# Where the products of a two-layer diffusion backbone stand in PSUM: pairs for gate and up, single banks for the rest

## The chip, the cores and the metric

The kernel runs on one core of one Trainium2 chip. The metric is the device time of one execution in microseconds (us). Before the change three runs gave 3039.61, 3045.07 and 3048.42 us, a median of 3045.07 us. The engines are TensorE (PE, with its weight loads as PEld), VectorE (DVE), ScalarE (ACT), GpSimd (POOL) and SyncE (SP, which issues DMAs).

## The reference

Two layers over 512 latent tokens (X) and 256 context tokens (C) of width 1024, in fp32. Each layer: a half-step SwiGLU feed-forward (FFN), a token mixer, a second FFN. Layer 0 mixes by a gated convolution and a Fourier transform, layer 1 by attention, in which only X goes on after.

```python
def macaron_ffn(h, m, g, w_in, w_out, slot):
    xm = modulate(h, g[2 * slot], m[:, :, 3 * slot], m[:, :, 3 * slot + 1])   # rmsnorm, scale, shift
    y = swiglu(xm, w_in, w_out)            # (silu(x @ w_gate) * (x @ w_up)) @ w_out, D_FF = 2816
    return h + FFN_RES * m[:, :, 3 * slot + 2] * rmsnorm(y, g[2 * slot + 1])
...
q_x = attn_queries(u[..., :Q_COLS], g_q_mla[o], w_uq[o], rope_da, rope_mla)
kv_x = attn_keys_values(u[..., Q_COLS:], g_kv_mla[o], w_uk[o], w_uv[o], rope_da, rope_mla)
kv_c = attn_keys_values(xc @ w_in[:, Q_COLS:], g_kv_mla[o], w_uk[o], w_uv[o], None, None)
```

## The kernel before

Activations lie feature by feature: a stream has eight tiles of 128 features by its tokens, X of 512 columns, C of 256. In the last FFN the two halves of X are streams of their own, A and B, of 256 columns. Every fp32 product is made of three matmuls on high and low parts (`mm3`, L212 to L214), and each weight tile is split into its high part on ScalarE (L140) and its low part on VectorE or GpSimd (L142).

PSUM has eight banks, given out by three pools: `mm`, three single banks (L103); `pr`, two pairs of banks (L109); `st`, one bank for sums (L106). A tile that asks for a bank of a full pool waits until the last reader of the oldest tile is done.

In an FFN the 22 feature tiles f are worked in six blocks. For each f, `gate_up` (L393) makes a gate and an up product, 48 matmuls, and `activated` (L413) turns them into an act: silu on ScalarE (L416), the product on VectorE (L417), then the split into a high part on ScalarE (L219) and a low part on VectorE (L220), which is the last reader of the banks. X's two products take a `pr` pair. C's, A's and B's take the two halves of one `mm` bank, except in the leading tiles. `out_proj` (L474) makes a block's share of the down projection in `mm` banks, copied by ScalarE (L488) in block 0 and added by VectorE (L490) later. Acts have five buffers per stream. In three of the four FFNs (`AHEAD` 4) one stream makes the acts of f = 0 to 5 before the other begins, and `out_proj` of block 0 follows both, so that the sixth act, f = 5, waits for a buffer that block 0 frees.

Between the layers' parts, `post` (L309) adds the normed result to the stream and `pre` (L292) makes the modulated rows for the next part, one row for each of the eight tiles. `scratch` (L226) gives each row its place in PSUM: an `mm` bank for lane c (C and B), halves of a `pr` pair for lane x (X and A). A row of `pre` is one step on VectorE (L303), one on ScalarE (L304) and one on VectorE (L305). `lead4` (L422) then starts the next FFN on the first two feature tiles as the rows come.

In the attention layer `latents` makes the low-rank queries (`q_lat`), the queries of group 0 (`da_qk(0, "q")`), the low-rank keys (`kv_lat`, which needs C's rows) and more. The work of groups 1 to 3 is laid between the steps of the attention of the group before, by gaps of a set length (`GAP`).

The program is written by generators that advance with TensorE's work; a scheduler then sets the order on each engine, and each engine runs its instructions in that order. The adaLN products (L366) are put on VectorE beside the FFNs.

Of the kernel before, what the change touches and what calls it, by code (L numbers as in the profile page):

```python
# [18 lines left out]
P = 128  # L19
D = 1024  # L20
KT = D // P
# [8 lines left out]
LEAD = 2  # L30
# [9 lines left out]
LEAD0 = 2  # L40
# [35 lines left out]
class Builder:  # L76
# [149 lines left out]
    def scratch(self, s, k, keep=False):  # L226


        if s.lane == "c":
            return self.mm()[:, :s.n]  # L230
        if k == 0 or k % 2 == 0 and not keep:
            s.scr = self.pr()
        return s.scr[:, k % 2 * 512:k % 2 * 512 + s.n]
# [58 lines left out]
    def pre(self, s, st, A, B):  # L292

        nc = self.nc
        rb = yield from self.rnorm(s, st, D)
        with self.tc.high_priority(PRIORITY):
            s.xm = [self.pre_tile(s, k, A, B, rb) for k in range(KT)]

    def pre_tile(self, s, k, A, B, rb):
# [9 lines left out]
    def post(self, s, st, A, want_stats=True):  # L309
# [6 lines left out]
        for k in range(KT):  # L316
            with self.tc.high_priority(PRIORITY):
                t = self.scratch(s, k)
# [103 lines left out]
    def lead4(self, s, ws, lead=None):  # L422
# [6 lines left out]
        lead = lead or LEAD  # L429
# [6 lines left out]
    def lead_gate_up(self, s, ws, acts, lead=None):  # L436
        pss = self.lead4(s, ws, lead)
        for f in range(2):
            self.act(s, f, pss[2 * f], pss[2 * f + 1], acts)
# [54 lines left out]
    def ffn(self, l, i, s0, s1, done, ahead=0, extra=False):  # L494
# [23 lines left out]
        if ahead:  # L518
            for s in both:
# [3 lines left out]
                else:  # L523
                    items.append((gu(0) + gu(1), lambda *ws, s=s: self.lead_gate_up(s, ws, acts, LEAD0)))
# [249 lines left out]
    def da_qk(self, g, which):  # L774
# [14 lines left out]
        def both(wa, wb):  # L789
            pa, pb = self.proj(X, [(wa, P, 0), (wb, P, 0)], KT, X.xm)  # L790
# [37 lines left out]
    def latents(self):  # L828
# [48 lines left out]
        items += self.da_qk(0, "q")  # L877
# [336 lines left out]
    def attention(self, X, C, A, B, close_xm, done):  # L1214
# [61 lines left out]
        for g in range(1, 4):  # L1276
            items += self.da_qk(g, "q") + self.da_qk(g, "k") + self.da_v(g)
# [31 lines left out]
def body(tc, io, stop=99):  # L1309
    nc = tc.nc  # L1310
    with ExitStack() as es:
# [92 lines left out]
        def step(l, slot, l2, slot2):  # L1404
            def gen(s, st):
                b.norms += 1
                new = yield from b.post(s, st, b.par[l, cname[s], 3 * slot + 2])
                yield from b.pre(s, new, b.par[l2, cname[s], 3 * slot2 + 1], b.par[l2, cname[s], 3 * slot2])
# [63 lines left out]
        items += b.mixer(X, C, step(0, 1, 0, 2))  # L1472
# [5 lines left out]
        if stop > 3:  # L1478
            items += b.ffn(1, 0, X, C, step(1, 0, 1, 1), AHEAD2)
        if stop > 4:  # L1480
# [11 lines left out]
            items += b.attention(X, C, A, B, close_xm, step(1, 1, 1, 2))  # L1492
# [139 lines left out]
```

## Time and profile before

| | |
|---|---|
| median of three runs | 3045.07 us |
| profiled execution | 3044.23 us, span 3042.4 us |
| PE busy | 2895.1 us, 95% |
| DVE, ACT, POOL busy | 54%, 35%, 27% |
| share of PE in the chain of waits | 80% |

The trace's names leave the buffer numbers out: `pr<-xm` is a product into a pair, `mm<-act` a down projection. "Idle before" is the time for which an engine stood still ahead of an instruction, and what ended it. The stages: ffn(0,0) to about 610 us, the mixer to 880, ffn(0,1) to 1455, ffn(1,0) to 2030, attention to 2625, the last FFN to the end.

### The profile page before, as it was taken

The page shows a single profiled execution, that of the slowest core. Times are in us where ns is not written, and L with a number is a line of the kernel's source. Part 1 is how long each engine was busy: PE and PEld are TensorE (multiplying, and loading weights), DVE is VectorE, ACT ScalarE, POOL GpSimd, SP SyncE. Part 2 cuts the span into 40 slices and gives each one's busy share as a digit, 9 for nine tenths or more (in the row PEclk, how much of TensorE's full clock was granted, in tenths as well). Part 3 has the DMA queues.
Part 4 walks back from the last instruction along what each step waited for, and adds up shares of the span by engine and source line. Part 5 has one row for each costly group of instructions (what it writes and reads, how often), then busy time and mean ns, then how long its engine had stood idle before and what let it go on. Part 6 is the DMA issues. An engine that isn't in the chain of part 4 may idle for free.

```text
span 3042.4 us, 44263 instructions
## 1 busy us (share of the span) xinstructions
PE 2895.1 (95%) x17842; PEld 2559.9 (84%) x17842; DVE 1652.7 (54%) x3026; ACT 1049.8 (35%) x1740; POOL 812.8 (27%) x439
## 2 busy tenths in 40 slices
PE   5899999999999999999999999997999999989998
PEld 4788888878888888888788888886798878889998
DVE  7865665675475434345745333366367757623335
ACT  5332112444343221124421122244355556542223
POOL 4221111332242111114311111142433422622122
PEclk9999999999999999999999999998999999999999
DMA  7743333333234322233333333352876674532224
GB/s 260 238 154 129 121 130 127 126 101 123 106 140 146 111 90 91 90 113 117 118 126 110 131 111 125 104 158 97 270 173 182 175 188 102 182 125 91 98 98 139
DMA packets 189807, 412.14 MB, mean 135 GB/s; under 512 B 58337, under 2 KB 83553, under 8 KB 189602
## 3 DMA queue, kind: packets, MB, share of 16 engines
q1 hardware_dynamic: 126642, 372.05, 36.5%
q0 software_dynamic: 62960, 37.27, 5.7%
q8 instruction: 140, 2.29, 0.3%
q14 instruction: 65, 0.53, 0.1%
HBM read 374.09 MB, written 35.00 MB: 134 GB/s over the span
## 4 chain that ended last, share of the span: by engine, by line
PE 80%; DVE 7%; issue 4%; DMA 4%; ACT 3%; POOL 2%; SPq 0%; ACTq 0%; DVEq 0%; POOLq 0%
PE mm L212 17%; PE mm L213 16%; PE mm L214 16%; PE pr L213 9%; PE pr L214 9%; PE pr L212 9%; DVE junk L366 1%; PE pr L997 1%; ACT wh L140 1%; DMA dr<-stg 1%; PE mm L1006 1%; DVE wl L142 1%; POOL wl L142 1%; DVE xm L305 1%; DMA ot<-dr 1%
## 5 line engine op out<-in xcount | busy, mean ns | idle before, releaser
L142 POOL TENSOR_TENSOR wl<-wraw,wh 128x1024 fp32r<-128x1024 f32 (+1 forms) x274 | 666.3, 2435 | 1966.4 <-ACT wh L140 1928.2
L140 ACT ACTIVATE wh<-wraw 128x1024 fp32r<-128x1024 f32 (+2 forms) x474 | 492.2, 1040 | 979.2 <-PE mm L213 664.7
L212 PE MATMUL mm<-xm,wh 128*128 128x256 f32 (+1 forms) x1992 | 588.3, 297 | 22.9 <-DVE xm L305 9.0
L214 PE MATMUL mm<-xm,wl 128*128 128x256 f32 (+1 forms) x1992 | 589.5, 296 | 9.4 <-DVE wl L142 9.4
L213 PE MATMUL mm<-xm,wh 128*128 128x256 f32 (+1 forms) x1992 | 588.6, 295 | 0.0
L213 PE MATMUL pr<-xm,wh 128*128 128x512 f32 (+1 forms) x1328 | 510.2, 384 | 17.3 <-POOL xm L1446 9.6
L212 PE MATMUL pr<-xm,wh 128*128 128x512 f32 (+1 forms) x1328 | 507.8, 383 | 14.8 <-ACT xm L304 7.7
L214 PE MATMUL pr<-xm,wl 128*128 128x512 f32 (+1 forms) x1328 | 506.4, 381 | 3.7 <-POOL wl L142 3.7
L212 PE MATMUL mm<-act,wh 128*128 128x256 f32 (+1 forms) x1408 | 459.2, 327 | 17.0 <-ACT y L488 11.6
L213 PE MATMUL mm<-act,wh 128*128 128x256 f32 (+1 forms) x1408 | 457.3, 325 | 0.2
L214 PE MATMUL mm<-act,wl 128*128 128x256 f32 (+1 forms) x1408 | 456.9, 325 | 0.0
L212 PEld LDWEIGHTS mm<-xm,wh 128*128 128x128 f32 x1992 | 377.5, 190 | 36.4 <-DVE xm L305 9.5
L214 PEld LDWEIGHTS mm<-xm,wl 128*128 128x128 f32 x1992 | 377.3, 189 | 18.9 <-DVE wl L142 10.0
L213 PEld LDWEIGHTS mm<-xm,wh 128*128 128x128 f32 x1992 | 379.3, 190 | 11.1 <-DVE xm L305 2.1
L366 DVE CUSTOM_DVE_ANT_0 junk<-wmod,cond 128x1024 bf16<-128x1024 f32 x256 | 374.8, 1464 | 6.4 <-DMA wmod<-in_w_mod_dram 4.2
L142 DVE TENSOR_TENSOR wl<-wraw,wh 128x1024 fp32r<-128x1024 f32 x200 | 251.1, 1255 | 227.6 <-ACT wh L140 224.9
L213 PEld LDWEIGHTS pr<-xm,wh 128*128 128x128 f32 x1328 | 252.3, 190 | 76.0 <-DVE xm L305 15.7
L212 PEld LDWEIGHTS pr<-xm,wh 128*128 128x128 f32 x1328 | 252.4, 190 | 71.7 <-ACT xm L304 15.8
L212 PEld LDWEIGHTS mm<-act,wh 128*128 128x128 f32 x1408 | 266.4, 190 | 48.4 <-ACT y L488 17.2
L214 PEld LDWEIGHTS pr<-xm,wl 128*128 128x128 f32 x1328 | 252.5, 190 | 53.9 <-POOL wl L142 4.1
L213 PEld LDWEIGHTS mm<-act,wh 128*128 128x128 f32 x1408 | 268.9, 191 | 25.4 <-DVE act L220 1.7
L214 PEld LDWEIGHTS mm<-act,wl 128*128 128x128 f32 x1408 | 266.8, 189 | 23.5
(241 smaller groups left out, 3467.8 us busy)
## 6 DMA issues: line engine op xcount, KB each, us to landing
wraw<-in_w_ffn_in_dram SPq DMA_DIRECT2D x250, 512.0 KB, 3.5
wmod<-in_w_mod_dram SPq DMA_DIRECT2D x160, 512.0 KB, 3.8
wraw<-in_w_ffn_out_dram SPq DMA_DIRECT2D x104, 512.0 KB, 3.5
dr<-stg SPq DMA_DIRECT2D x40, 512.0 KB, 3.5
wraw<-in_w_in_even_dram SPq DMA_DIRECT2D x32, 512.0 KB, 3.5
qs<-dr POOLq DMA_DIRECT2D x56, 256.0 KB, 12.0
dr<-stg SPq DMA_DIRECT2D x36, 256.0 KB, 6.3
ks<-dr POOLq DMA_DIRECT2D x24, 384.0 KB, 10.8
```

The source lines that it names most:

```text
L140: self.nc.scalar.activation(out=h, in_=r, func=AF.Copy)
L142: eng.tensor_tensor(out=l, in0=r, in1=h.bitcast(F32), op=ALU.subtract)
L212: mmul(out, w[0], x[0], start=first, stop=False)
L213: mmul(out, w[0], x[1], start=False, stop=False)
L214: mmul(out, w[1], x[0], start=False, stop=last)
L305: nc.vector.scalar_tensor_tensor(out=x[:, 1], in0=t, scalar=B[:, k:k + 1], in1=x[:, 0].bitcast(F32), op0=ALU.add, op1=ALU.subtract)
L366: dot = nc.vector.tensor_tensor_reduce(out=junk, in0=w, in1=self.cond[n], op0=ALU.mult, op1=ALU.add, scale=1.0, scalar=0.0, accum_out=par[ ...
L997: self.nc.tensor.matmul(ps[:, c0:c1], q, k[:, c0:c1], start=i == 0, stop=i == len(passes) - 1)
L1006: self.nc.tensor.transpose(ps[:, kt * P:(kt + 1) * P], w[:, (k0 + kt) * P:(k0 + kt + 1) * P], self.ident)
```

## The change

It has four parts.

1. `gate_up` takes a `pr` pair for every stream.
2. `scratch` gives a row an `mm` bank by default; one pair for all eight rows is taken only in the posts of X after the mixer, of C after ffn(1,0) and of A after the attention, and in the pres of X and C after ffn(1,0).
3. `lead4` takes the first two feature tiles interleaved: tile 0 row by row, with the first three rows of tile 1 laid between, where before it made tile 0 whole and then tile 1.
4. The queries of group 1 are made right behind those of group 0, ahead of `kv_lat`, and both are projected into a `pr` pair (the last argument of `proj`).

```diff
-LEAD = 2
+LEAD = 3
...
-LEAD0 = 2
...
-    def scratch(self, s, k, keep=False):
-        if s.lane == "c":
+    def scratch(self, s, k, pair):
+        if not pair:
             return self.mm()[:, :s.n]
-        if k == 0 or k % 2 == 0 and not keep:
+        if k == 0:
             s.scr = self.pr()
         return s.scr[:, k % 2 * 512:k % 2 * 512 + s.n]
...
-        t = self.scratch(s, k, True)
+        t = self.scratch(s, k, pair)
...
     def gate_up(self, s, f, ws, acts):
         nc = self.nc
-        if s.n == 512:
-            ps = self.pr()
-            g, u = ps[:, :512], ps[:, 512:]
-        else:
-            ps = self.mm()
-            g, u = ps[:, :s.n], ps[:, s.n:2 * s.n]
+        ps = self.pr()
+        g, u = ps[:, :s.n], ps[:, 512:512 + s.n]
...
-        for i in range(0, 4, lead):
-            for k in range(KT):
-                for o, w in zip(pss[i:i + lead], ws[i:i + lead]):
-                    self.mm3(o, self.wk(w, k), s.xm[k], k == 0, k == KT - 1)
+        order = [(0, 0)]
+        for k in range(1, KT):
+            order += [(0, k)] + ([(2, k - 1)] if k <= LEAD else [])
+        order += [(2, k) for k in range(LEAD, KT)]
+        for i, k in order:
+            for o, w in zip(pss[i:i + 2], ws[i:i + 2]):
+                self.mm3(o, self.wk(w, k), s.xm[k], k == 0, k == KT - 1)
...
-            pa, pb = self.proj(X, [(wa, P, 0), (wb, P, 0)], KT, X.xm)
+            pa, pb = self.proj(X, [(wa, P, 0), (wb, P, 0)], KT, X.xm, which == "q" and g < 2)
...
-        items += self.da_qk(0, "q")
+        items += self.da_qk(0, "q") + self.da_qk(1, "q")
...
-            items += self.da_qk(g, "q") + self.da_qk(g, "k") + self.da_v(g)
+            items += (self.da_qk(g, "q") if g > 1 else []) + self.da_qk(g, "k") + self.da_v(g)
...
-        def step(l, slot, l2, slot2):
+        def step(l, slot, l2, slot2, posts=(), pres=()):
...
-        items += b.mixer(X, C, step(0, 1, 0, 2))
+        items += b.mixer(X, C, step(0, 1, 0, 2, (X,)))
...
-            items += b.ffn(1, 0, X, C, step(1, 0, 1, 1), AHEAD2)
+            items += b.ffn(1, 0, X, C, step(1, 0, 1, 1, (C,), (X, C)), AHEAD2)
...
-            items += b.attention(X, C, A, B, close_xm, step(1, 1, 1, 2))
+            items += b.attention(X, C, A, B, close_xm, step(1, 1, 1, 2, (A,)))
```

The order on the engines shows what becomes of this. On TensorE, C's six products in ffn(0,1): names with `pr` are pairs, with `mm` single banks, and the number tells tiles apart; `[waits ...]` names the engines waited for. Before:

```order
4875 L212 MATMUL pr_8210<-xm_7904,wh_8125 128x256 [waits DVE_49]
...
4923 L212 MATMUL mm_8344<-xm_7904,wh_8320 128x256 [waits Activation_49]
...
4936 L212 MATMUL pr_8211<-xm_7904,wh_8198 128x256 [waits DVE_49]
...
5019 L212 MATMUL mm_8417<-xm_7904,wh_8332 128x256 [waits Activation_49]
...
5067 L212 MATMUL mm_8484<-xm_7904,wh_8405 128x256 [waits Activation_49]
...
5115 L212 MATMUL mm_8551<-xm_7904,wh_8472 128x256 [waits DVE_49,Activation_49]
...
5163 L212 MATMUL mm_8626<-act_7846,wh_8539 128x512 [waits DMAHW4_49,DVE_49,Activation_49]
```

and now:

```order
4877 L211 MATMUL pr_8225<-xm_7919,wh_8140 128x256 [waits DVE_49]
...
4925 L211 MATMUL pr_8226<-xm_7919,wh_8213 128x256 [waits DVE_49]
...
4973 L211 MATMUL pr_8359<-xm_7919,wh_8335 128x256 [waits DVE_49]
...
5021 L211 MATMUL pr_8432<-xm_7919,wh_8347 128x256 [waits DVE_49]
...
5069 L211 MATMUL pr_8499<-xm_7919,wh_8420 128x256 [waits DVE_49]
...
5117 L211 MATMUL mm_8641<-act_7861,wh_8554 128x512 [waits DMAHW4_49,Activation_49]
...
5130 L211 MATMUL pr_8566<-xm_7919,wh_8487 128x256 [waits DVE_49]
...
5178 L212 MATMUL mm_8663<-act_7861,wh_8554 128x512
```

Before, C's third to sixth products stood in `mm` banks and the third began ahead of the second's; now the six are in pairs and each begins with a wait for VectorE, and the sixth has moved behind the first down projections.

On VectorE, the rows of X's `pre` in front of ffn(1,0): `h` is the stream, `xm` the row. Before:

```order
1422 L303 SCALAR_TENSOR_TENSOR pr_12240<-h_109,par_7946,st_12234 128x512 [waits PE_49]
...
1425 L305 SCALAR_TENSOR_TENSOR xm_12239<-pr_12240,par_9214,xm_12239 128x512 [waits Activation_49]
1426 L303 SCALAR_TENSOR_TENSOR pr_12240<-h_111,par_7946,st_12234 128x512 [waits DVE_49]
1427 L305 SCALAR_TENSOR_TENSOR xm_12244<-pr_12240,par_9214,xm_12244 128x512 [waits Activation_49]
1428 L303 SCALAR_TENSOR_TENSOR pr_12240<-h_113,par_7946,st_12234 128x512 [waits DVE_49]
1429 L305 SCALAR_TENSOR_TENSOR xm_12248<-pr_12240,par_9214,xm_12248 128x512 [waits Activation_49]
```

and now:

```order
1417 L301 SCALAR_TENSOR_TENSOR mm_12259<-h_109,par_7961,st_12253 128x512 [waits PE_49]
1418 L301 SCALAR_TENSOR_TENSOR mm_12264<-h_111,par_7961,st_12253 128x512 [waits DVE_49]
...
1420 L303 SCALAR_TENSOR_TENSOR xm_12258<-mm_12259,par_9229,xm_12258 128x512 [waits Activation_49]
1421 L303 SCALAR_TENSOR_TENSOR xm_12263<-mm_12264,par_9229,xm_12263 128x512 [waits Activation_49]
1422 L301 SCALAR_TENSOR_TENSOR mm_12269<-h_113,par_7961,st_12253 128x512 [waits DVE_49]
1423 L301 SCALAR_TENSOR_TENSOR mm_12274<-h_115,par_7961,st_12253 128x512 [waits DVE_49]
```

The first step of a row (written to `pr` before, to an `mm` tile of its own now) and its last step alternated; now two first steps stand ahead of two last ones.

On TensorE, the entry of the attention layer: `xm_16951` and `xm_16981` are X's first row, `xm_17338` and `xm_17360` C's. Before:

```order
11031 L212 MATMUL mm_17238<-xm_16951,wh_17025 128x512 [waits DVE_49]
...
11061 L212 MATMUL mm_17302<-xm_16951,wh_17220 128x512
...
11089 L212 MATMUL mm_17417<-xm_16951,wh_17226 128x512 [waits DVE_49]
...
11113 L212 MATMUL mm_17442<-xm_16951,wh_17232 128x512 [waits DVE_49]
...
11137 L212 MATMUL mm_17475<-xm_17338,wh_17226 128x256 [waits DVE_49]
```

and now:

```order
11037 L211 MATMUL pr_17262<-xm_16981,wh_17055 128x512
...
11061 L211 MATMUL pr_17262<-xm_16981,wh_17244 128x512 [waits Activation_49]
...
11085 L211 MATMUL mm_17511<-xm_16981,wh_17420 128x512 [waits Activation_49]
...
11111 L211 MATMUL mm_17536<-xm_16981,wh_17426 128x512 [waits Activation_49]
...
11141 L211 MATMUL mm_17569<-xm_17360,wh_17420 128x256 [waits Activation_49]
...
11155 L211 MATMUL pr_17432<-xm_16981,wh_17250 128x512 [waits DVE_49]
...
11203 L212 MATMUL mm_17569<-xm_17369,wh_17420 128x256 [waits DVE_49]
```

The queries of group 0 (mm_17238, mm_17302; now pr_17262) no longer begin with a wait for VectorE, `kv_lat` on X (mm_17417; now mm_17511) follows at once, and the queries of group 1 (pr_17432) stand among the products of C's rows.

## Rows read from the trace of the kernel before

**Rows 1.** Parts 1 and 4 of the page, whole span: busy time and share of TensorE, and the share of the chain of waits by engine.

```profile
PE 2895.1 (95%) x17842; PEld 2559.9 (84%) x17842; DVE 1652.7 (54%) x3026; ACT 1049.8 (35%) x1740; POOL 812.8 (27%) x439
...
PE 80%; DVE 7%; issue 4%; DMA 4%; ACT 3%; POOL 2%; SPq 0%; ACTq 0%; DVEq 0%; POOLq 0%
```

**Rows 2.** One line's instructions (L212, the first of the three matmuls of a product), two stretches: name, count, duration in ns (min/median/max), first and last start. The first stretch is one 256-column pair of C or B size, the second one 512-column pair of X; each pair has 48 matmuls, 16 of them on this line.

```profile
L212 PE MATMUL mm<-xm,wh x16: 276/276/276, 2690.3 to 2695.4; 128*128 128x256 f32 x16
...
L212 PE MATMUL pr<-xm,wh x16: 390/392/404, 466.7 to 477.2; 128*128 128x512 f32 x16
```

**Rows 3.** Groups by line and shape on TensorE, 1100 to 1450 us (the middle of the second feed-forward layer): count | busy us, mean ns of one | idle us before them.

```profile
L212 PE MATMUL pr<-xm,wh 128*128 128x512 f32 x202 | 79.7, 395 | 0.0
...
L212 PE MATMUL mm<-xm,wh 128*128 128x256 f32 x208 | 58.7, 282 | 0.0
```

**Rows 4.** Windows: stretch in us, its length, then busy us (and count) of PE, PEld, DVE, ACT, POOL, then granted TensorE clock, DMA share, GB/s.

```profile
115.60:163.00 47.40, 38.27 (x295) 37.65 (x294) 41.38 (x60) 17.05 (x25) 15.46 (x6) 0.89 0.66 222
...
610.00:650.00 40.00, 34.09 (x184) 25.87 (x183) 29.63 (x79) 18.48 (x33) 14.32 (x6) 1.00 0.29 93
955.60:993.00 37.40, 35.41 (x291) 34.71 (x290) 17.25 (x20) 15.68 (x23) 14.82 (x6) 1.00 0.44 153
...
1457.00:1490.00 33.00, 30.59 (x119) 22.09 (x120) 23.88 (x60) 13.85 (x23) 7.83 (x4) 0.95 0.14 49
...
2056.00:2108.00 52.00, 34.96 (x173) 29.34 (x172) 30.12 (x88) 19.43 (x38) 15.07 (x9) 0.80 0.20 71
...
2184.00:2196.00 12.00, 6.33 (x23) 4.41 (x23) 3.54 (x5) 3.80 (x6) 4.56 (x4) 0.72 1.18 311
2624.00:2662.00 38.00, 34.72 (x266) 31.64 (x265) 26.79 (x79) 22.01 (x40) 22.57 (x10) 1.00 0.43 145
2661.00:2707.00 46.00, 41.78 (x348) 41.08 (x347) 21.40 (x35) 21.58 (x34) 16.95 (x7) 0.96 0.48 164
2706.00:2732.00 26.00, 18.96 (x105) 16.27 (x105) 2.44 (x4) 8.63 (x21) 2.37 (x1) 0.80 0.25 81
```

**Rows 5.** The last step of an activation (L220, it frees the product's banks), 110 to 182 us: name, count, duration, first and last start, forms.

```profile
L220 DVE TENSOR_TENSOR act<-pr,act x4: 411/554/692, 112.1 to 176.8; 128x512 fp32r<-128x512 f32 x2, 128x256 fp32r<-128x256 f32 x2
```

**Rows 6.** Timeline, 961 to 965.2 us, the eviction of C's first pair in the second feed-forward layer: start us, duration us, engine, line, operation [idle before <-releaser].

```profile
961.21 0.28 PE L214 MATMUL pr<-xm,wl 128*128 128x256 f32 x1
...
962.36 0.37 ACT L416 ACTIVATE ta<-pr 128x256 f32<-128x256 f32 x1
962.48 1.23 DVE L142 TENSOR_TENSOR wl<-wraw,wh 128x1024 fp32r<-128x1024 f32 x1 [4.56 <-ACT wh L140]
...
963.63 0.42 DVE L417 TENSOR_TENSOR pr<-ta,pr 128x256 f32<-128x256 f32 x1
...
964.08 0.39 ACT L219 ACTIVATE act<-pr 128x256 fp32r<-128x256 f32 x1 [0.41 <-DVE pr L417]
...
964.50 0.42 DVE L220 TENSOR_TENSOR act<-pr,act 128x256 fp32r<-128x256 f32 x1 [0.45 <-ACT act L219]
...
965.17 0.28 PE L212 MATMUL pr<-xm,wh 128*128 128x256 f32 x1
```

**Rows 7.** Waits of TensorE by what ended them, 115 to 180 us: us in total, times, longest us.

```profile
PE mm L214 <- DVE wl L142: 8.4, 1, 8.4
```

**Rows 8.** Timeline of VectorE, 138 to 143 us: the adaLN product (L366) that runs beside the feed-forward layer.

```profile
138.39 1.22 DVE L366 CUSTOM_DVE_ANT_0 junk<-wmod,cond 128x1024 bf16<-128x1024 f32 x1
...
139.71 1.22 DVE L366 CUSTOM_DVE_ANT_0 junk<-wmod,cond 128x1024 bf16<-128x1024 f32 x1
```

**Rows 9.** Windows of TensorE round two waits: length, busy us (count), granted clock, DMA share, GB/s. The first and third stretch each hold a wait, the second and fourth what follows it.

```profile
854.40:857.40 3.00, 0.07 (x2) 0.94 0.50 168
857.40:860.50 3.10, 3.10 (x14) 0.50 0.02 7
2677.90:2679.90 2.00, 0.28 (x4) 1.00 0.36 143
2679.90:2683.00 3.10, 3.10 (x27) 1.00 0.59 196
```

**Rows 10.** Timeline of VectorE, 1458.5 to 1464 us: the norm rows of X in front of ffn(1,0), with X's rows in one bank pair.

```profile
1459.30 0.75 DVE L305 SCALAR_TENSOR_TENSOR xm<-pr,par,xm 128x512 fp32r<-128x512 f32 x1 [0.76 <-ACT xm L304]
...
1461.60 0.75 DVE L305 SCALAR_TENSOR_TENSOR xm<-pr,par,xm 128x512 fp32r<-128x512 f32 x1 [0.76 <-ACT xm L304]
```

**Rows 11.** Timeline of VectorE, 2626.3 to 2630 us: the norm rows of A in front of the last feed-forward layer.

```profile
2626.63 0.48 DVE L305 SCALAR_TENSOR_TENSOR xm<-pr,par,xm 128x256 fp32r<-128x256 f32 x1
...
2628.18 0.48 DVE L305 SCALAR_TENSOR_TENSOR xm<-pr,par,xm 128x256 fp32r<-128x256 f32 x1 [0.54 <-ACT xm L304]
```

**Rows 12.** Waits of TensorE, 2624 to 2735 us (start of the last feed-forward layer): us in total, times, longest us.

```profile
PE mm L212 <- ACT y L488: 7.0, 12, 1.4
PE pr L214 <- POOL wl L142: 3.7, 2, 1.9
```

**Rows 13.** Waits of TensorE, 1457 to 1530 us (start of ffn(1,0)).

```profile
PE mm L212 <- ACT y L488: 4.0, 2, 2.4
```

**Rows 14.** Waits of TensorE, 2050 to 2110 us (entry of the attention layer).

```profile
PE mm L212 <- DVE xm L305: 9.0, 1, 9.0
PE mm L212 <- DVE ssum L243: 8.0, 1, 8.0
```

**Rows 15.** Groups by line and shape on TensorE, 2191 to 2211 us, while the first head is attended: count | busy us, mean ns | idle us before them. The row is of group 1's query projection.

```profile
L212 PE MATMUL mm<-xm,wh 128*128 128x512 f32 x18 | 7.7, 425 | 0.0
```

More of the change, by code (lines that the diff above doesn't have):

```diff
@@ L290, in kept, with pre @@
         return r
-    def pre(self, s, st, A, B):
+    def pre(self, s, st, A, B, pair=False):
         nc = self.nc
@@ L296, in pre, with pre_tile @@
         with self.tc.high_priority(PRIORITY):
-            s.xm = [self.pre_tile(s, k, A, B, rb) for k in range(KT)]
-    def pre_tile(self, s, k, A, B, rb):
+            s.xm = [self.pre_tile(s, k, A, B, rb, pair) for k in range(KT)]
+    def pre_tile(self, s, k, A, B, rb, pair=False):
         nc = self.nc
         x = self.xmpool.tile([P, 2, s.n], F32R, name=self.nm("xm"), tag=f"xm{s.name}{k}", bufs=1)
-        t = self.scratch(s, k, True)
+        t = self.scratch(s, k, pair)
         nc.vector.scalar_tensor_tensor(out=t, in0=s.h[k], scalar=A[:, k:k + 1], in1=rb, op0=ALU.mult, op1=ALU.mult)
@@ L307, in pre_tile, with post @@
         return x[:, 0], x[:, 1]
-    def post(self, s, st, A, want_stats=True):
+    def post(self, s, st, A, want_stats=True, pair=False):
         nc = self.nc
@@ L317, in post @@
             with self.tc.high_priority(PRIORITY):
-                t = self.scratch(s, k)
+                t = self.scratch(s, k, pair)
                 nc.vector.scalar_tensor_tensor(out=t, in0=y[k], scalar=A[:, k:k + 1], in1=rb,
@@ L420, in activated, with lead4 @@
         acts[s, f] = (a[:, 0], a[:, 1])
-    def lead4(self, s, ws, lead=None):
+    def lead4(self, s, ws):
         self.finish(s.ready)
@@ L428, in lead4, with lead_gate_up @@
             pss += [ps[:, :s.n], ps[:, 512:512 + s.n]]
-        lead = lead or LEAD
-        for i in range(0, 4, lead):
-            for k in range(KT):
-                for o, w in zip(pss[i:i + lead], ws[i:i + lead]):
-                    self.mm3(o, self.wk(w, k), s.xm[k], k == 0, k == KT - 1)
-        return pss
-    def lead_gate_up(self, s, ws, acts, lead=None):
-        pss = self.lead4(s, ws, lead)
+        order = [(0, 0)]
[5 more added lines that the diff above has]
+                self.mm3(o, self.wk(w, k), s.xm[k], k == 0, k == KT - 1)
+        return pss
+    def lead_gate_up(self, s, ws, acts):
+        pss = self.lead4(s, ws)
         for f in range(2):
@@ L523, in ffn @@
                 else:
-                    items.append((gu(0) + gu(1), lambda *ws, s=s: self.lead_gate_up(s, ws, acts, LEAD0)))
+                    items.append((gu(0) + gu(1), lambda *ws, s=s: self.lead_gate_up(s, ws, acts)))
                 for f in range(3 if six else 2, 2 + ahead):
@@ L1402, in body @@
         b.close_pre, b.close_attn = close_pre, close_attn
-        def step(l, slot, l2, slot2):
+        def step(l, slot, l2, slot2, posts=(), pres=()):
             def gen(s, st):
                 b.norms += 1
-                new = yield from b.post(s, st, b.par[l, cname[s], 3 * slot + 2])
-                yield from b.pre(s, new, b.par[l2, cname[s], 3 * slot2 + 1], b.par[l2, cname[s], 3 * slot2])
+                new = yield from b.post(s, st, b.par[l, cname[s], 3 * slot + 2], pair=s in posts)
+                yield from b.pre(s, new, b.par[l2, cname[s], 3 * slot2 + 1], b.par[l2, cname[s], 3 * slot2],
+                                 s in pres)
                 b.norms -= 1
```

## The prediction

> **What bounds the kernel now.** I read the engine part of the page first, then the chain of waits [rows 1]: TensorE is busy 95% of the span and holds 80% of the chain. VectorE, next in line, is at 54%. So TensorE's work sets the time, and a change that adds and removes no matmul can move only two things: the time TensorE stands still, about 147 us, and the time it runs at a lower clock. Then I read where these lie. In the middle of a feed-forward layer no group of products has idle time before it [rows 3]; there the plan of PSUM costs nothing now. What is lost lies where stages meet, in windows of 26 to 52 us [rows 4]. Last I read the pace of products [rows 2]: one product (three matmuls) of 256 columns takes 5.4/16 = 0.34 us, so one matmul 0.113; of 512 columns 0.70 and 0.233. A pair of products is 5.4 us for C, A or B and 11.2 us for X. A window's length less its matmuls at this pace is what it loses.
>
> **Part 1, pairs for C in the first two leading phases.** With AHEAD 4, X's sixth act finds no buffer until block 0 of `out_proj` has run, and its products hold their pair until then: of the four last splits between 110 and 182 us, two have 512 columns (X's), and the last of all starts at 176.8, when C's are long under way [rows 5]. C's six pairs, which now all want `pr`, have one pair of banks between them. Each product must wait for the eviction of the one before. Before, they also had three `mm` banks.
>
> What one such eviction takes stands once in the trace, since C's first tiles used `pr` already. In ffn(0,1) the last matmul ends at 961.49; silu, product, two splits and the hand-overs end at 964.92, 3.43 us later, and TensorE begins again at 965.17, 3.68 after its last matmul [rows 6]. Of this VectorE's weight split of 1.23 stood in front of the product. The four steps by themselves are 0.37 + 0.42 + 0.39 + 0.42 = 1.6, with the two hand-overs of 0.41 and 0.45 2.5 us. Another bad case is two adaLN products of 1.22 each on VectorE between the steps [rows 8], 2.45 more. I take 3.5, the one that was measured, with 2.5 and 5.9 as ends.
>
> ffn(0,0): before, the window 115.6 to 163 has 47.4 us for 295 matmuls of 0.113, 33.4, so 14.0 are lost, clock 0.89 among it [rows 4]. One wait of 8.4, for a weight split behind VectorE's queue, is most of that [rows 7]. After: the first eviction is behind the same queue, 8.4 + 3.5 + 0.7 for the restart = 12.6; three more at 3.5 are 10.5; the fifth is covered by down projections that now stand before the sixth product; and half of the clock's loss (0.11 of 47.4 is 5.2) stays, 2.6. Sum 25.7, so **+11.7**.
>
> ffn(0,1): 37.4 us for 291 matmuls, 33.0: 4.4 lost [rows 4]. After: four evictions at 3.5 in the open, 14.0, so **+9.6**.
>
> **Part 1 in the last FFN.** Here A and B both have a sixth act that holds a pair, but before, `out_proj` copies and their products shared `mm`: 7.0 us of waits for copies and 3.7 for weight splits [rows 12]. B's stretch loses 46.0 - 348 x 0.113 = 6.6 and, from 2706 to 2732, 26.0 - 105 x 0.113 = 14.1, together 20.7 [rows 4]. After: four evictions in the open, 14.0, and what is left of the copies and splits, 1.5 + 1.9: 17.4. The copies have three `mm` banks for themselves. **-3.3**. Behind it, and in ffn(1,0) (AHEAD2 is 1, so no act holds a pair for long), block 0 has the banks alone too; of 4.0 us of waits [rows 13] I take **-3.5**. Later blocks: a C product on `pr` has two pairs and X's 11.2 us between, an eviction 2.5 to 3.7; so no wait, 0.
>
> **Parts 2 and 3, rows and leads.** When X's rows stand in one pair, VectorE's last step waits 0.76 us for ScalarE and a row comes every 2.30 us [rows 10]. With a bank per row, first and last steps go two by two, as the order shows, and the wait is covered: 2 x 0.75 = 1.51 a row. Eight rows save 6.3. TensorE can gain no more than it loses: idle 5.9 in 610 to 650 and 33.0 - 119 x 0.233 = 5.2 in 1457 to 1490 [rows 4]. At each I take **-5** (0 to -5.9). At the mixer's end three of C's output tiles stand behind the rows and eat the gain: **0** (-6.3 to +5, half of an X pair). For A, the row step of 1.55 [rows 11] falls to 0.97 by the same sum, and three rows of tile 1 lie between those of tile 0, so TensorE has twice the work per early row. The window 2624 to 2662 loses 38.0 - 266 x 0.113 = 7.9 [rows 4]; I take **-6** (-2 to -7.9).
>
> **Part 4, entry of the attention.** Before, two waits of 9.0 and 8.0 us [rows 14] are all of the 17.0 idle us of 2056 to 2108, and clock 0.80 costs 0.2 x 35 = 7 [rows 4]: 24 lost. Now the queries of group 0 and `kv_lat` on X follow at once, and 11.2 us of group 1's queries stand among the products of C's rows. But C's rows, post and pre, now share one pair, like X's of [rows 10], and come later; I leave 8 of wait and 4 of clock: -12. What is taken away is filler. Group 1's queries ran while the first head was attended, with no idle time before them [rows 15]; just before, from 2184 to 2196, TensorE is busy 6.3 of 12 us with DMA at 1.18 [rows 4]. A quarter of the 11.2 back as idle is 3. **-9** (0 to -17).
>
> **The clock.** New short waits number 3 + 4 + 4 = 11. A wait of 3 us at 854.4 is followed by 3.1 us at a granted clock of 0.50 (1.2 of 2.4 GHz), 1.55 us lost; a wait of 2 us at 2677.9 is followed by full clock [rows 9]. At 3.5 us I let half of the eleven fall: 5.5 x 1.55 = **+8.5** (0 to 17.1). By the Trainium skill (TensorE: Matmul & The Clock Gate, section "A second HAM failure mode: psum-queue depth-cycling"), a TensorE that idles briefly between matmul groups as it cycles through PSUM has its clock go back and forth and pays in every burst; by that all eleven would cost, and the sum would be 8.5 higher. The trace agrees at the one wait and not at the other. The same notes (Perfetto Trace Analysis, section "Optimizing Tensor Performance") want independent groups to rotate through several banks so that one's eviction lies beside the next one's matmuls; that speaks against part 1 wherever one pair is left, and the estimate of 3.5 us per product is what it would cost here.
>
> **Sum.** 11.7 + 9.6 - 3.3 - 3.5 - 5 - 5 + 0 - 6 - 9 + 8.5 = -2.0. The profiled execution took 3044.23 us (span 3042.4 and 1.8 around it), 0.8 below the median of 3045.07; the difference is the same for both kernels, so the forecast is 3045.07 - 2.0 = 3043: two opposite groups of some 30 us each that nearly cancel.
>
> **Rivals.** *Short evictions* (3024). VectorE's splits do not stand in the way, an eviction takes 2.5 as its parts add up: 11 x 1.0 = -11; waits of that length keep the clock, like the one of 2 us [rows 9]: -8.5. 3043 - 19.5 = 3024. For it: VectorE is at 54%, and in 955.6 to 993 it is busy 17.3 of 37.4 [rows 4]. Against: the only eviction measured had a split in front.
>
> *Crowded evictions* (3064, slower). Two adaLN products of VectorE fall between the steps of five of them, 5 x 2.45 = +12.3, and the clock falls after every wait, +8.5. 3043 + 20.8 = 3064. Its place is C's six products in the first two leading phases; it decides once a wait there exceeds about 5 us. For it: VectorE is busy 41.4 of 47.4 us in 115.6 to 163 [rows 4]. Against: the rate in the other two phases, about half.
>
> *The attention gives it back* (3052). The part that moved changes nothing, since the first head waits for transfers in any case, and TensorE's idle time goes to where the filler was: the -9 is 0. For it: DMA share 1.18 beside TensorE at half [rows 4]. Against: the waits at the entry are VectorE's alone [rows 14].
>
> *The change doesn't do what it says*: C's products are given out in another order, so no pair is short. The order shows every one of the six beginning with a wait for VectorE; I give it nothing.
>
> **How the numbers follow.** Forecast 0.45 (its own range 3030 to 3055, from the bounds of the terms taken as independent), short evictions 0.25, crowded 0.18, attention 0.12. Within 0.3%, 9 us, is about what a measurement of this kernel can't tell from no change: 3036 to 3054. Faster is a third of the forecast (0.15) and nearly all of short evictions: 0.39. Slower is all of crowded, a tenth of the forecast and a few in a hundred of the attention: 0.24. The rest, 0.37, is the same. The range reaches from 3018 to 3064: it leaves out a third of short evictions and half of crowded, under 2 in 10.
>
> **What would show it.** Right: in 121 to 181 and 961 to 1018 waits of `pr` products for VectorE's last split, some 3.5 us each, eleven in the three phases; waits for the copies of `out_proj` gone in the last FFN and ffn(1,0); the row step of X at 1.5 us; one wait of about 8 instead of 9.0 and 8.0 at the attention's entry. Wrong: waits of `pr` products that are absent (then a pair was free, and the sum falls by 30), longer than 5 us (crowded), a granted clock of 1.00 through the first two leading phases (then the 8.5 is 0), a middle of a layer that has idle time before its products, or a stretch 2184 to 2211 with several us more idle than before (the attention rival).

## The result and the profile after

The change made the kernel slower: a median of 3076.85 us (3073.61 to 3081.23) against 3042.34 us of the kernel before on the same chip, a ratio of 1.0123 with a 95% interval of 1.0101 to 1.0145. By the ratio that is about 37 us (the medians lie 34.5 apart); 3043 was forecast, and 3064 was the end of the range. One execution of run 12 below, 4701.69 us at a granted clock of 0.557, is left out there. The profiled execution took 3073.61 us with a span of 3071.8. The engine part of its page answers to [rows 1]:

```profile
PE 2900.9 (94%) x17842; PEld 2574.3 (84%) x17842; DVE 1644.2 (54%) x3026; ACT 1045.6 (34%) x1740; POOL 815.4 (27%) x439
```

The work is the same and the span 29.4 us longer. To find where, I laid the two traces over each other at equal work: each matmul counts as much as its columns, and for a time in the trace of before I took the time when the changed kernel had done as much. There is one trace of each kernel.

| time before, us | changed kernel later by | what lies in the step |
|---|---|---|
| 115 | 1.9 | |
| 200 | 22.3 | first leading phase: +20.4 |
| 610, 850 | 21.2, 16.0 | X's rows ahead of the mixer: -5.2 |
| 950 | 27.1 | mixer's end, X's rows: +11.1 |
| 1020 | 45.1 | second leading phase: +18.0 |
| 1455, 2000 | 45.8, 35.6 | start of ffn(1,0): -10.2 |
| 2180 | 31.8 | entry of the attention: -3.8 |
| 2200 | 24.0 | -7.8: by here the kernel before has stood still for the first head, the changed one not yet |
| 2600, 2625 | 37.5, 43.8 | attention, with that wait: +13.5, then A's rows: +6.3 |
| 2740 | 39.8 | first acts of the last FFN: -4.0 |
| 3000 | 29.8 | rest of the last FFN: -10.0 |

**The leading phases.** Windows of the changed kernel (columns as in [rows 4]); the first and third hold as many matmuls as 115.6 to 163 and 955.6 to 993 there, the second is the mixer's end.

```profile
117.50:187.20 69.70, 44.60 (x295) 42.74 (x294) 39.17 (x57) 17.76 (x26) 16.07 (x6) 0.80 0.47 161
885.00:907.50 22.50, 9.65 (x36) 8.10 (x37) 16.48 (x34) 7.23 (x11) 0.65 (x1) 0.55 0.16 56
982.80:1041.00 58.20, 43.57 (x291) 42.02 (x290) 15.54 (x21) 17.02 (x25) 14.22 (x6) 0.85 0.33 109
```

295 matmuls take 69.7 us instead of 47.4, and 291 take 58.2 instead of 37.4. Of these, 16 and 13 have 512 columns here and 7 and 3 before, which makes some 1.1 and 1.2 us of the difference. TensorE's waits in these two phases, and from 2700 to 2760:

```profile
PE pr L211 <- DVE act L219: 25.1, 5, 12.1
...
PE pr L211 <- DVE act L219: 14.6, 4, 5.8
...
PE pr L211 <- DVE act L219: 11.8, 4, 3.2
```

These are the forecast waits of a product for the last split of the one before, at the forecast places. The longest but one is opened up by VectorE's and ScalarE's timeline, 143.8 to 148.5 us, the eviction of C's second pair:

```profile
143.88 1.23 DVE L141 TENSOR_TENSOR wl<-wraw,wh 128x1024 fp32r<-128x1024 f32 x1 [6.20 <-ACT wh L139]
...
145.02 0.42 DVE L411 TENSOR_TENSOR pr<-ta,pr 128x256 f32<-128x256 f32 x1
...
145.35 3.21 DVE L364 CUSTOM_DVE_ANT_0 junk<-wmod,cond 128x1024 bf16<-128x1024 f32 x1
145.47 0.39 ACT L218 ACTIVATE act<-pr 128x256 fp32r<-128x256 f32 x1 [0.41 <-DVE pr L411]
...
148.49 0.41 DVE L219 TENSOR_TENSOR act<-pr,act 128x256 fp32r<-128x256 f32 x1
```

An adaLN product, here 3.21 us long, stands between product and split, which is the crowded case of the rivals. The waits aren't the whole. With the 512-column matmuls at 0.233 us and the others at 0.113, the first phase has 35.3 us of work, so 34.4 of its 69.7 are lost, 9.3 more than the waits; the second has 34.4, so 23.8 of its 58.2 are lost, 9.2 more. Most of that is the clock. Three stretches of the first phase, length, then TensorE's busy time (count), granted clock, DMA share, GB/s:

```profile
125.90:139.50 13.60, 4.17 (x19) 0.50 0.73 249
146.40:153.20 6.80, 4.24 (x20) 0.50 0.62 221
160.00:163.40 3.40, 3.40 (x16) 0.50 0.74 264
```

With the stretch at 170.3 that is 15.2 us of work at a clock of 0.50, of which half, 7.6 us, is lost; in the second phase it is 15.0 and 7.5. The wait that ends at 170.1 is 2.7 us long; the window with it and the one behind:

```profile
166.90:170.10 3.20, 0.51 (x6) 0.31 (x4) 0.85 (x2) 1.71 (x3) 1.61 (x1) 1.00 0.51 164
170.30:173.60 3.30, 3.30 (x17) 3.30 (x17) 0.00 (x0) 0.00 (x0) 0.54 (x1) 0.50 0.41 150
```

By the granted clock in the trace each of the twelve waits of 2.7 us and more (four in each of these three stretches) has a stretch at 0.50 (1.2 GHz) in it or right behind it. The Trainium skill (TensorE: Matmul & The Clock Gate, section "A second HAM failure mode: psum-queue depth-cycling") tells of a kernel whose TensorE idles briefly between groups of matmuls as it cycles through PSUM banks, often enough that its clock goes back and forth, at a cost between the bursts; here the trace agrees, twelve times of twelve. Not every wait of this length does it: one of 2.69 us that ends at 714.7 before the change has a clock of 1.00 behind it, and so has one of 2.69 that ends at 158.3 in run 13.

**Rows.** VectorE's first step of a row in X's post after the mixer (L319 before, L317 now) and in A's after the attention; count, duration, first and last start. Before:

```profile
L319 DVE SCALAR_TENSOR_TENSOR pr<-y,par,st x8: 743/750/756, 842.1 to 862.6; 128x512 f32<-128x512 f32 x8
...
L319 DVE SCALAR_TENSOR_TENSOR pr<-y,par,st x8: 483/486/490, 2604.1 to 2614.0; 128x256 f32<-128x256 f32 x8
```

and now:

```profile
L317 DVE SCALAR_TENSOR_TENSOR pr<-y,par,st x8: 743/750/755, 857.9 to 885.4; 128x512 f32<-128x512 f32 x8
...
L317 DVE SCALAR_TENSOR_TENSOR pr<-y,par,st x8: 480/490/490, 2641.4 to 2658.7; 128x256 f32<-128x256 f32 x8
```

Seven steps in 20.5 us before and 27.5 now, and in 9.9 and 17.3: the post took a new pair every second row, and now keeps one for all eight. So X's sum of squares is done 7 us later, when C's last projections no longer cover it; TensorE's waits from 880 to 950 us:

```profile
PE st L254 <- DVE ssum L241: 4.4, 1, 4.4
PE mm L211 <- DVE xm L303: 4.0, 1, 4.0
PE st L260 <- DVE rs L281: 2.4, 1, 2.4
```

**The attention.** The waits of 9.0 and 8.0 us at the entry [rows 14] are gone; these are the longest from 2030 to 2140 us now:

```profile
PE mm L211 <- ACT xm L302: 2.8, 4, 1.1
PE st L260 <- DVE t L743: 2.6, 1, 2.6
```

Yet the entry gains only 3.8 us by the mark of 2180. One thing that eats the gain is the clock, which is at 0.50 through this stretch with 10.7 us of work in it (columns as in [rows 4]):

```profile
2119.30:2132.90 13.60, 10.67 (x31) 8.62 (x32) 9.98 (x19) 4.83 (x10) 5.09 (x4) 0.50 0.17 63
```

The step to 2200 is no gain. Both kernels wait for the transfers of the first head, the one before from 2184.8 to 2190.8 us of its time, the changed one from 2228 to 2234 of its own, which is behind 2200 at equal work. TensorE's waits from 2150 to 2310 us before:

```profile
PE pr L997 <- DMA qs<-dr: 3.3, 2, 3.2
PE pr L997 <- DMA dr<-stg: 2.4, 1, 2.4
```

and from 2182 to 2346 us now, when group 1's queries are missing beside the first head:

```profile
PE pr L994 <- DMA qs<-dr: 4.2, 2, 3.7
PE pr L994 <- ACT e L986: 3.6, 2, 2.3
```

From 2180 to 2600 the attention loses 5.7 us.

**The rest of the last FFN.** Here both kernels keep TensorE busy without a gap at a granted clock of 1.00, and yet 100 us hold 852 matmuls before (first fence) and 885 now (second):

```profile
2760.00:2860.00 100.00, 100.00 (x852) 100.00 (x851) 29.76 (x54) 27.68 (x42) 21.59 (x9) 1.00 0.28 93
```

```profile
2780.00:2880.00 100.00, 100.00 (x885) 100.00 (x884) 33.44 (x62) 27.30 (x39) 21.60 (x9) 1.00 0.28 96
```

That is a pace of 0.117 and 0.113 us. Runs 11 and 8 below, two variants of the changed kernel, have one each, so the plan of the pairs alone doesn't set it; whether the change brought these 10 us isn't shown. Without them the traces differ by 39.

### The profile page after: what moved, and what is told of

It reads as the page before. It is cut to its first block, busy times and chain, and to the rows that moved or that the text cites. A ratio compares the mean times of both kernels' runs of the same rounds, so it can differ in the third digit from the quotient of the medians.

```text
span 3071.8 us, 44215 instructions
## 1 busy us (share of the span) xinstructions
PE 2900.9 (94%) x17842; PEld 2574.3 (84%) x17842; DVE 1644.2 (54%) x3026; ACT 1045.6 (34%) x1740; POOL 815.4 (27%) x439
## 5 line engine op out<-in xcount | busy, mean ns | idle before, releaser
L211 PE MATMUL pr<-xm,wh 128*128 128x256 f32 (+1 forms) x2960 | 979.4, 331 | 63.4 <-DVE act L219 52.4
L212 PE MATMUL pr<-xm,wh 128*128 128x256 f32 (+1 forms) x2960 | 978.9, 331 | 8.4 <-POOL xm L1445 7.9
L213 PE MATMUL pr<-xm,wl 128*128 128x256 f32 (+1 forms) x2960 | 978.6, 331 | 1.8 <-POOL wl L141 1.8
L139 ACT ACTIVATE wh<-wraw 128x1024 fp32r<-128x1024 f32 (+2 forms) x474 | 492.1, 1040 | 1049.8 <-PE mm L212 464.6
L211 PEld LDWEIGHTS pr<-xm,wh 128*128 128x128 f32 x2960 | 569.9, 193 | 123.9 <-DVE act L219 56.0
L212 PEld LDWEIGHTS pr<-xm,wh 128*128 128x128 f32 x2960 | 569.8, 193 | 64.8 <-POOL xm L1445 10.5
L213 PEld LDWEIGHTS pr<-xm,wl 128*128 128x128 f32 x2960 | 569.9, 193 | 53.5 <-POOL wl L141 2.0
L212 PE MATMUL mm<-act,wh 128*128 128x256 f32 (+1 forms) x1408 | 452.9, 322 | 0.0
L411 DVE TENSOR_TENSOR pr<-ta,pr 128x256 f32<-128x256 f32 (+1 forms) x175 | 92.1, 527 | 495.2 <-ACT ta L410 494.9
L211 PEld LDWEIGHTS mm<-act,wh 128*128 128x128 f32 x1408 | 264.1, 188 | 31.8 <-ACT act L218 3.2
L212 PEld LDWEIGHTS mm<-act,wh 128*128 128x128 f32 x1408 | 265.2, 188 | 24.2 <-DVE act L219 0.6
L487 DVE TENSOR_TENSOR y<-y,mm 128x256 f32<-128x256 f32 (+1 forms) x320 | 165.6, 520 | 214.1 <-PE mm L213 211.9
L410 ACT ACTIVATE ta<-pr 128x256 f32<-128x256 f32 (+1 forms) x175 | 78.8, 451 | 404.3 <-PE pr L213 404.3
L219 DVE TENSOR_TENSOR act<-pr,act 128x256 fp32r<-128x256 f32 (+1 forms) x175 | 91.3, 522 | 81.0 <-ACT act L218 80.4
L211 PE MATMUL mm<-xm,wh 128*128 128x512 f32 (+1 forms) x360 | 126.7, 356 | 4.6 <-ACT xm L302 2.8
L213 PE MATMUL mm<-xm,wl 128*128 128x512 f32 (+1 forms) x360 | 125.9, 351 | 3.4 <-POOL wl L141 3.4
## 6 DMA issues: line engine op xcount, KB each, us to landing
ks<-dr POOLq DMA_DIRECT2D x24, 384.0 KB, 10.5
```

Source lines behind the costliest of these rows:

```text
L139: self.nc.scalar.activation(out=h, in_=r, func=AF.Copy)
L211: mmul(out, w[0], x[0], start=first, stop=False)
L212: mmul(out, w[0], x[1], start=False, stop=False)
L213: mmul(out, w[1], x[0], start=False, stop=last)
L219: self.nc.vector.tensor_tensor(out=lo, in0=src, in1=hi.bitcast(F32), op=ALU.subtract)
L410: nc.scalar.activation(out=t, in_=g, func=AF.Silu)
```

## The experiments

My theory after the result: X's held pair leaves C one pair, so that evictions lie in the open (part 1, +38 with the clock); one pair for a whole post makes rows late (part 2, +11 and +6); and group 1's queries only shift time (part 4). The main rival is VectorE's queue, with any number of pairs. The kernel before, measured beside them each time, had medians from 3034 to 3042 us; so runs are compared by their ratio to it. A step "at equal work" is a difference of two entries of a table like the one above.

**Run 1. Part 1 undone.** `gate_up` as in the diff's removed lines.

> The changed kernel with C's, A's and B's gate and up products back in the two halves of one mm bank (part 1 undone, parts 2 to 4 kept). Held-pair theory (C's six products share the one pair that X's sixth act leaves free): the waits of pr products for the last split between 120 and 182 us and between 990 and 1030 us vanish with the clock that falls after them, 20 us in ffn(0,0) and 18 in ffn(0,1); the last feed-forward layer gives back 3 to 8. Sum 30 to 35 us below the changed kernel, 3042 to 3047. Rival (the plan of the rows, not that of the products, costs the time): under 10 us.

Measured: 3046.8 us, ratio 1.0043 (1.0025 to 1.0061), 0.8% below the changed kernel. The steps of +20.4 and +18.0 become -1.2 and +0.4; the mixer's end keeps its loss. So products, not rows, cost the leading phases their time. By the ratios the gain is 24 us, less than the 30 to 35 expected: 1020 to 2000 takes 2.0 us off instead of 9.5, and the rest of the last FFN runs at the slower of the two paces.

**Run 2. Six act buffers, pairs kept.**

```diff
-        a = self.ffpool.tile([P, 2, s.n], F32R, ..., bufs=5)
+        a = self.ffpool.tile([P, 2, s.n], F32R, ..., bufs=6 if s.name in "xa" else 5)
```

The adaLN loads that borrow X's buffers follow.

> The changed kernel with six buffers for the acts of X and A, so that the sixth act finds one and gives its pair back; products stay in pairs. Held-pair theory: C has two pairs in turn, 5.4 us of products beside an eviction of some 3 us; the waits go except behind the first, long one in ffn(0,0); 30 to 38 us less in the first two phases and up to 10 less in the last feed-forward layer: 3030 to 3045. Rival (evictions are long since VectorE's queue holds adaLN products and weight splits, with any number of pairs): waits of 3 us and more stay, under 15 us gained.

Measured: 3015.45 us, ratio 0.9926 (0.9902 to 0.9951): faster than both kernels and below what was expected. The surplus lies in the last FFN's first acts (2665 to 2740), which take some 20 us less at equal work than in the changed kernel, where up to 10 was expected: A's sixth act, too, had held a pair. TensorE's waits in 110 to 190 and in 2620 to 2750 us; in 930 to 1030 none of this kind is left:

```profile
PE pr L211 <- DVE act L219: 9.0, 2, 5.4
...
PE pr L211 <- DVE act L219: 0.9, 2, 0.8
```

With every step of the eviction as before and only the held pair given back, 14.6 and 11.8 us of waits go. The rival falls, but for the 9.0 us in the first phase.

**Run 3. X's post on alternating pairs.** `scratch` takes a new pair at even rows there, as before the change.

> The changed kernel, but X's rows in the post after the mixer take a new pair every second row, as in the kernel before. One-pair theory: the row step falls from 3.9 to 2.9 us, the norm sums of X come 7 us earlier, beside C's last projections, and the 11 us lost between 880 and 910 us come back: 3064 to 3068. Rival (that loss comes from C's projections having moved ahead, or from the row plan of pre): no change, 3077.

```profile
L317 DVE SCALAR_TENSOR_TENSOR pr<-y,par,st x8: 740/750/756, 856.4 to 876.1; 128x512 f32<-128x512 f32 x8
```

The row step is 19.7/7 = 2.8 us again, and the mixer's end loses 2.6 us at equal work instead of 11.1. The time, 3068.08 us, ratio 1.0111 (1.0069 to 1.0152), doesn't separate from the changed kernel's: the step is shown by the trace alone.

**Run 4. Part 4 undone.**

> The changed kernel with part 4 undone: group 1's queries back in their place beside the first head, projections in mm banks. Theory from the two traces (the entry gains 11 us and the attention gives 12 back between 2200 and 2300 us): within 4 us of the changed kernel, 3073 to 3081, the entry to the attention 8 to 12 us longer and the stretch to 2340 us as much shorter. Rival (the forecast's term: the move gains 9): 3086.

Measured: 3068.42 us, ratio 1.0108 (1.0073 to 1.0144), which doesn't separate from the changed kernel's. At equal work the entry (2000 to 2180) takes 2.4 us off instead of 3.8, and 2180 to 2600 adds 0.7 instead of 5.7. By the traces the move gains little at the entry, and the first heads give more than that back. The 11 and 12 us of the expectation come from the mark of 2200, between the two kernels' waits for the first head.

**Run 5. The pair free after the product (C, A, B).**

```diff
-        nc.vector.tensor_tensor(out=u, in0=t, in1=u, op=ALU.mult)
+        p = u if s.n == 512 else t
+        nc.vector.tensor_tensor(out=p, in0=t, in1=u, op=ALU.mult)
...
-        self.split(u, a[:, 0], a[:, 1])
+        self.split(p, a[:, 0], a[:, 1])
```

> The changed kernel, but the product silu(g) x u of C, A and B is written to SBUF in place of the pair, so that a pair is free after the product and not after the two splits; X as it was, its sixth act still holds a pair. By the timeline of the changed kernel the product of C's second eviction ends 3.5 us before its last split, those of the others 0.9 to 1.5 us: the four waits in ffn(0,0) go from 12.1, 5.8, 3.1, 2.7 to 10.6, 2.3, 2.2, 1.8 and in ffn(0,1) from 3.5, 5.8, 2.7, 2.7 to 2.6, 2.3, 1.8, 1.8: 12 to 13 us less wait in the two phases, some 4 in the last feed-forward layer. Clock theory (a wait of some 2 us leaves the granted clock at 1.00, one of 2.7 lowers it): the drops to 0.50 behind all but the first wait go too, 12 to 16 us more, together about 30 below the changed kernel: 3047. Rival (the clock falls behind any wait of this kind): 16 us, 3061.

Measured: 3050.79 us, ratio 1.0044 (1.0025 to 1.0064), 0.8% below the changed kernel. The waits in 110 to 190 and, with those of other kinds left out, in 880 to 1040 us, and the window behind a wait of 2.31 us that ends at 980.1:

```profile
PE pr L211 <- DVE ta L412: 17.1, 4, 11.0
...
PE pr L211 <- DVE ta L412: 8.2, 4, 2.3
```

```profile
980.20:983.50 3.30, 3.30 (x16) 3.30 (x17) 1.87 (x1) 0.31 (x1) 1.93 (x1) 0.50 0.66 173
```

The waits shrink by 14.4 us, but the clock falls behind those of 2.31 too, and behind two of the four of 1.8 to 2.0, so the clock theory as I put it is wrong: the length of a wait alone doesn't tell. The two phases lose 10.6 and 9.8 us instead of 20.4 and 18.0, nearer to the rival. Most of what else the run gained lies in the last FFN, where A's held pair is freed too, which I had not allowed for.

**Run 6. Part 1 alone, on the kernel before.**

> The kernel before with part 1 alone: gate_up takes a pair for every stream. Held-pair theory: the two leading phases lose 20 + 18 us as in the changed kernel and the last feed-forward layer wins back up to 8 (there the leads still are those of before): 3064 to 3078 beside 3040 for the kernel before. Rival (parts 2 and 3 make the phases worse, through other starting times): under 3055.

Measured: 3096.32 us, ratio 1.0178 (1.0145 to 1.0212), worse than expected by 20. The phases cost 20.8 and 17.8 at equal work, as in the changed kernel. The extra lies at the ends of the layers, +5.5 (200 to 610), +4.2 (1020 to 1455) and +6.5 (2000 to 2030). There X's rows and C's last products both want pairs, which I take for the cause (at 621 us a product of C waits 2.7 us for a split); the changed kernel, with its rows in `mm` banks, has none of it, -1.1, +0.7 and -0.5.

**Run 7. Six buffers and X's post on alternating pairs.**

> The changed kernel with six act buffers for X and A and X's post after the mixer on alternating pairs. If the two losses are separate, they add: what six buffers gave (3015) less 6 to 9 us for the row step: 3006 to 3010. Rival (with the pairs free sooner, the norm chain of X is hidden anyway): 3015.

Measured: 3009.91 us, ratio 0.9904 (0.9878 to 0.993); the mixer's end costs 6.2 us at equal work where six buffers alone had 10.6 (run 8, the same code up to there, has 3.8: one trace says no more than that). As expected in size, but the intervals overlap.

**Run 8. The same with part 4 undone.**

> As the run with six buffers and alternating pairs, and part 4 undone as well. Theory (part 4 only shifts time from the entry to the first head): within 4 us of that run. Rival (the fourth run beside the changed kernel, 3068 against 3077, says that undoing it gains): 5 to 9 us less.

Measured: 3008.75 us, ratio 0.9901 (0.987 to 0.9931): no difference.

**Run 9. Six buffers, on the kernel before.**

> The kernel before with six act buffers for X and A and nothing else. There C's third to sixth products stand in mm banks, and only its second pair waits. Theory (six buffers are worth much only where the products stand in pairs): 3 to 8 us less than before, 3030 to 3035. Rival (the held pair cost the kernel before as much, and the whole gain of the second run is the buffer's): 20 us less or more, 3020 and below.

Measured: 3027.31 us, ratio 0.9955 (0.9937 to 0.9973), 14 us: more than expected, less than the rival. At equal work 12.8 of it lie in the last FFN's first acts (2665 to 2740), where A's held pair cost the kernel before too.

**Run 10. Six buffers, alternating pairs in X's and A's posts.**

> The changed kernel with six act buffers for X and A and alternating pairs in both X's post after the mixer and A's post after the attention (part 4 kept). A's row step was 1.41 us in the kernel before and is 2.47 in the changed one; seven steps are 7.4 us, all of them ahead of the last feed-forward layer. Theory: the 5 to 6 us lost in 2600 to 2625 come back, 3003 to 3006 where X's post alone gave 3010. Rival (other work of the attention covers A's rows): 3010.

```profile
L317 DVE SCALAR_TENSOR_TENSOR pr<-y,par,st x8: 482/486/490, 2592.2 to 2602.1; 128x256 f32<-128x256 f32 x8
```

Measured: 3003.96 us, ratio 0.9878 (0.9858 to 0.9898). A's step is 9.9/7 = 1.41 us as before, and 2600 to 2625 loses 0.3 us instead of 6.3. The interval overlaps that of run 7, so this gain, too, is shown by the trace alone.

**Run 11. The same with part 4 undone.**

> The same with part 4 undone, in the same call. Part 4 gains some 11 us at the attention's entry in every trace that has it and gives 12 to 13 back by the second group. Theory: within 4 us of the run before it, 3000 to 3008, with no gain at the entry and no loss behind it. Rival (the trace of the eighth run, 15 us shorter than that of the seventh): undoing it gains 8 or more.

Measured: 3003.46 us, ratio 0.9877 (0.9858 to 0.9896). Part 4 is worth nothing that can be told, and this and the run before are the best, 1.2% under the kernel before. The 11 us expected at the entry are again those of the mark of 2200: by 2180 run 10 has gained 4.6 us since 2000 and this one 5.1.

Run 8 and this one differ in A's post alone, and show both paces in the last FFN, at no waits and full clock. Run 8's window, then this one's:

```profile
2700.00:2800.00 100.00, 100.00 (x885) 100.00 (x884) 33.01 (x63) 26.85 (x40) 21.57 (x9) 1.00 0.30 96
```

```profile
2700.00:2800.00 100.00, 100.00 (x852) 100.00 (x851) 32.05 (x60) 25.57 (x37) 21.66 (x9) 1.00 0.29 92
```

**Run 12. Products to SBUF for every stream, on top of it.**

> The same with the product silu(g) x u of every stream written to SBUF, so that pairs are free after the product. If the pairs still hold anything up with six buffers, it is the first eviction of C in ffn(0,0) behind VectorE's adaLN products (waits of 9.0 us in two): 2 to 4 us less. Rival (no product waits for a pair any more, and the two ta buffers, held longer, become the wait): the same or a few us more.

Measured: 3014.66 us, ratio 0.9899 (0.9876 to 0.9922). Not faster, as the rival said; whether slower, the intervals leave open, and why wasn't followed.

**Run 13. AdaLN products later.**

```diff
         def gen():
+            yield 160.0
             for w in work:
...
-                yield us / len(work)
+                yield (us - 160.0) / len(work)
```

> The changed kernel, but the adaLN products that are spread over a feed-forward layer begin 160 us later and then come the closer together, so that few stand on VectorE while C's first six products are evicted. Theory (the two long waits of 12.1 and 5.8 in ffn(0,0) and the one of 5.8 in ffn(0,1) hold adaLN products between the steps; the rest of each wait is the bare eviction of some 3 us): they fall to about 3 each, 12 us less wait and 5 to 8 less at half clock, 3057 to 3062; waits of 2.7 to 3.5 stay, so most of the loss stays. Rival (the held pair alone sets them, whatever VectorE does): waits as before, 3077.

Measured: 3059.58 us, ratio 1.0054 (1.0034 to 1.0073), 0.7% below the changed kernel. Waits in 110 to 190 and 960 to 1040 us:

```profile
PE pr L212 <- DVE act L220: 11.8, 4, 3.2
...
PE pr L212 <- DVE act L220: 12.0, 4, 3.5
```

25.1 and 14.6 became 11.8 and 12.0, none over 3.5. So some 16 us of the waits belong to VectorE's queue, and the bare eviction of 2.7 to 3.5 us stays, with the clock that falls behind seven of these eight waits.

**Run 14. Part 1 and six buffers, on the kernel before.**

> The kernel before with part 1 and six act buffers for X and A, nothing else: what pairs for C are worth where no act holds a pair. Held-pair theory: the 38 us of the two leading phases and the last layer's waits go, so at least 45 us below part 1 alone (3096). Whether it is below the kernel before with six buffers (3027) is open: the ends of ffn(0,0), ffn(0,1) and ffn(1,0), where C's last products and X's norm rows share the pairs, cost part 1 alone 6, 5 and 6 us and should still do so: 3025 to 3040. Rival (pairs are good by themselves, the rows' plan adds nothing): 3015 or less.

Measured: 3022.51 us, ratio 0.9936 (0.9917 to 0.9954): 74 us below part 1 alone, 2.4% in the ratios. Against six buffers without part 1 (0.9955) the intervals overlap: where no act holds a pair, part 1 by itself neither gains nor loses what can be told here. Its ends of the layers still cost 5.7, 6.6 and 7.3 us at equal work.

## Why the prediction was wrong

**The held pair and its waits: right.** Forecast were 12.6 + 10.5 = 23.1 us in ffn(0,0), 14.0 in ffn(0,1) and 14.0 in the last FFN; the trace has 25.1, 14.6 and 11.8. How the sum comes about was only half right: an eviction with the adaLN products away is 2.7 to 3.5, and three of the twelve waits hold such a product, as the crowded rival said, which gave its price to five.

**"At 3.5 us I let half of the eleven fall": wrong.** This is the term that was mis-sized most in part 1. The clock fell at all twelve, the stretches at 0.50 hold 3.4 to 4.8 us of work instead of the 3.1 of [rows 9], and beyond the waits the two phases lost 9.3 + 9.2 = 18.5 us, 15.1 of them by the clock, where 2.6 + 7 x 0.5 x 1.55 = 8.0 were forecast. I took one wait of 2 us at full clock as a rule. The stretch from 2677.9 to 2679.9 in [rows 9] holds a wait of only 1.72 us, and the same trace has one of 1.93 with the clock at 0.50 behind it (columns as in [rows 9]):

```profile
2663.40:2665.40 2.00, 0.07 (x2) 1.00 0.36 145
2666.10:2669.50 3.40, 3.40 (x18) 0.50 0.46 154
```

Run 5 shows the same behind waits of 2.31 us.

**"At the mixer's end ... 0": wrong, +11.1.** I worked out the rows of `pre` and not those of `post`, whose pairs the same edit of `scratch` took from a new one every second row to one for all. Run 3 puts the loss there. The same holds for A: its lead gave some 8 us (2625 to 2670), more than the 6 forecast, but the rows of its post cost 6.3 ahead of it. The products behind it cost some 4, where -3.3 and about 3 for the clock were forecast, so 2600 to 2740 came to +2.3. Alternating pairs take the 6.3 away.

**"-12" at the entry and "3" given back: both wrong.** By 2180 the entry gave -3.8, and from there to 2600 the attention took 5.7 back, together +1.9 where -9 was forecast. The rival that put the sum at 0 was right, as three pairs of kernels with and without part 4 agree. What else than the stretch at half clock keeps the entry from gaining its 12 wasn't followed.

**X's rows and the start of ffn(1,0): right.** -5.2 ahead of the mixer (forecast -5), -10.2 at ffn(1,0) (-5 and -3.5); the copies' wait of 4.0 [rows 13] is 0.6 now, the 7.0 of [rows 12] 0.4. In the middle of a layer nothing moved, 0.7 us from 1020 to 1455.

So most of the entry's minus term and all of that of the last FFN's products were not there, a term put at 0 was +11, and the plus term of the clock was too small, all on one side; that the gains and losses "nearly cancel" had hidden how one-sided the unknowns were. The crowded rival's 3064 was the nearest case. It had the clock right, gave five waits an adaLN product where three had one, and was short by the mixer's end and by the attention.

## What to carry to other kernels

Before a bank plan is changed, count for each phase who holds a buffer and why: a tile that waits for a buffer of another pool keeps its banks, and one buffer more (six acts) was worth 60 us here, more than the plan itself. Follow every caller of an allocation helper whose rule changes, not only the one that the change is about. And price a short wait of TensorE at one and a half times its length (the two phases lost 58.2 us to 39.7 us of waits and what lay behind them) as long as the trace doesn't show the clock to survive it at that place.

## What was not expected of the hardware

A stretch with TensorE busy throughout at a granted clock of 1.00 ran at two paces, 0.117 and 0.113 us per matmul of 256 columns, 852 or 885 in 100 us. Of the sixteen traces nine have the fast one through most of the last FFN and seven the slow one. The three kernels with C's, A's and B's products in `mm` banks (before, runs 1 and 9) have the slow one, but so have runs 6, 10, 11 and 12, whose products stand in pairs, while the changed kernel and the others have the fast one. Over some 260 us that is 10 us, as much as many an edit; what sets it stays open.
